# The first value product taken row tile by row tile of x, beside the norm of the next tile

## The chip, the cores and the metric

The kernel runs on one core of a Trainium2 chip. The metric is the device time of one execution in microseconds (us). Its engines are named as the profile names them: PE (TensorE, matmuls and transposes; PEld loads its weights), DVE (VectorE), ACT (ScalarE), POOL (GpSimd) and SP (SyncE, which here only issues transfers). Each engine runs its own queue in order, and waits at an instruction until the semaphores it needs have been raised.

## The reference

One decoder layer on x of 1024 tokens by 1024 features, in fp32. h = rms_norm(x) * pre_g; z = h @ w_in, whose columns are queries, keys, values and gates of 8 heads of differential attention (QA, KA, VA, GA) and of 4 heads of gated linear attention (QB, KB, VB, GB, and a narrow gate input); the two attentions; then out = x + rms_norm(mix @ w_out) * post_g. The change touches only the head of this: the norm of x, its transposition, and the first products of h with w_in.

```python
def hybrid_layer(x, layer_idx, pre_g, post_g, w_in, ...):
    h = rms_norm(x, pre_g)
    z = jnp.einsum('bsd,de->bse', h, w_in)
    qa, ka, va, ga, qb, kb, vb, gb, gk_low = split_columns(z)
    ...
```

## The kernel before

**Precision.** A matmul of two fp32 operands is done as three: each operand is split into a high part (rounded to the fast format, `hi`, by an ACT copy) and a rest (`lo`, by a DVE subtraction), and hi x hi, hi x lo and lo x hi are added in PSUM. So every weight block and every block of h passes ACT once and DVE once before PE may use it.

**Seven products for eight.** The product h @ w_in is done by a Strassen-like scheme on halves: seven products (numbers 1, 2, 6, 7, 5, 3, 4) of sums of blocks of h with sums of blocks of the weights. The blocks of h, all transposed so that features lie on partitions, are h11 (rows 0 to 511 of x, features 0 to 511), h12 (the same rows, features 512 to 1023), h22 (rows 512 to 1023, features 512 to 1023), and the sums s1 to s4. Product 1 needs h11, product 2 needs h12, product 6 needs s2, product 7 needs s3, product 5 s1, product 4 h22, product 3 s4.

**The order of work.** `order` lists the products by weight matrix: first the value matrix VB (512 columns at a time, called wide) in products 1 and 2, each in two steps kk over 256 features; then products 1 and 2 of three 256-column pairs of KA, QA (`EARLY`, their weights loaded at the head as `w_early`); then VB's products 6, 7, 5, 3, 4; then VA; then all else. `go(n)` takes the next n entries: it prepares the weights of the entries ahead (`prepare`, `make_weights`, `block_weights`) and issues the matmuls (`step`, `step_wide`, `multiply_wide`). A wide step is 24 matmuls of 128x512 into four PSUM banks, one for each row tile t of 128 tokens: 2 features blocks q by 3 terms j by 4 tiles.

**The head.** x lies in eight row tiles of 128 tokens. `norm_x(st)` for st 0 to 3 takes ACT's square with a sum, the inverse root (`rstd`: Ln and Exp on ACT, three small DVE steps), and the scaling of the tile by DVE (first half of the features) and POOL (second half). The four tiles' norms are issued one behind the other. `first(0)` transposes the first half of all four tiles on PE (16 transposes into four banks `xT`), and `put` makes h11's hi (ACT, times pre_g) and lo (DVE) from PSUM, 128x512 at a time; product 1 follows with all four row tiles for each feature block. `first(1)` does the same for h12. Tiles 4 to 7 are normed in pairs, scaled by POOL, and transposed in `blocks(j)`, four times, which makes h22, s2 and s3 for feature block j. `blocks` stands between steps of product 2 and of the first early pairs. POOL makes f1 (h11 and h12 in full precision, `f1hi` and `f1lo` in the profile), s1 and s4.

**What sets the order.** PE's instructions stay in program order (`mm`, `tr`). The instructions of other engines are placed by the framework's scheduler, unless `tc.keep_in_program_order` pins them or `tc.issue_after` puts them behind another. PSUM has eight banks, handed out by `take_bank` from the list `free` and given back in the order of release.

## Time and profile before

| | |
|---|---|
| median of 3 runs | 977.59 us (977.15 to 982.69) |
| the profiled execution | 977.73 us, span 976.0 us |
| PE busy | 956.0 us, 98% |
| DVE / ACT / POOL busy | 738.7 / 590.9 / 211.5 us |
| granted clock | 0.998 |

The span is the time from the first to the last recorded instruction; the execution's own time lies 1.7 us above it. A busy share is an average; where time can be won or lost is read from the stages: PE does its first transposes at 7.46 us, its first matmul at 13.71 us, and is then busy until the last slice.

### The profile page before, as it was taken

The page shows a single profiled execution, that of the slowest core. Times are in us where ns is not written, and L with a number is a line of the kernel's source. Part 1 is how long each engine was busy: PE and PEld are TensorE (multiplying, and loading weights), DVE is VectorE, ACT ScalarE, POOL GpSimd, SP SyncE. Part 2 cuts the span into 40 slices and gives each one's busy share as a digit, 9 for nine tenths or more (in the row PEclk, how much of TensorE's full clock was granted, in tenths as well). Part 3 has the DMA queues.
Part 4 walks back from the last instruction along what each step waited for, and adds up shares of the span by engine and source line. Part 5 has one row for each costly group of instructions (what it writes and reads, how often), then busy time and mean ns, then how long its engine had stood idle before and what let it go on. Part 6 is the DMA issues. An engine that isn't in the chain of part 4 may idle for free.

```text
span 976.0 us, 14803 instructions
## 1 busy us (share of the span) xinstructions
PE 956.0 (98%) x4866; PEld 806.1 (83%) x4866; DVE 738.7 (76%) x1450; ACT 590.9 (61%) x1152; POOL 211.5 (22%) x289
## 2 busy tenths in 40 slices
PE   6999999999999999999999999999999999999997
PEld 4888888878888888888888888788888888888875
DVE  6996476889889776778787766577787778887655
ACT  8641232347467467766677774357667667787764
POOL 5420100011211221112110000023232233443232
PEclk9999999999999999999999999999999999999999
DMA  8354643768865875899986569997575678995657
GB/s 306 99 152 153 212 134 98 217 174 270 265 240 194 268 250 192 265 280 304 315 278 183 180 204 346 376 337 233 164 252 185 189 267 246 331 262 104 194 157 156
DMA packets 144556, 220.37 MB, mean 226 GB/s; under 512 B 14704, under 2 KB 78704, under 8 KB 144384
## 3 DMA queue, kind: packets, MB, share of 16 engines
q1 hardware_dynamic: 130144, 175.38, 56.6%
q0 software_dynamic: 14336, 44.05, 15.1%
q8 instruction: 38, 0.62, 0.3%
q14 instruction: 38, 0.31, 0.1%
HBM read 133.93 MB, written 88.60 MB: 228 GB/s over the span
## 4 chain that ended last, share of the span: by engine, by line
PE 86%; DMA 6%; DVE 3%; ACT 3%; issue 1%; SPq 1%; DVEq 0%; POOL 0%; ACTq 0%
PE v L111 15%; PE x L111 15%; PE ypart L111 11%; PE y L111 10%; PE z L111 10%; PE sc L111 6%; PE po L111 5%; PE yps L111 4%; PE wtr L114 3%; PE gpo L111 2%; PE kv L111 1%; DMA m_raw<-mixd 1%; DMA m_lo<-mixe 1%; DMA mixd<-o 1%; DMA k_d<-qk_st 1%
## 5 line engine op out<-in xcount | busy, mean ns | idle before, releaser
L1177 ACT ACTIVATE p<-p,stt 128x896 f32<-128x896 f32 (+7 forms) x128 | 99.3, 777 | 46.7 <-DVE stt L1167 43.5
L335 DVE TENSOR_TENSOR w<-w_raw,w 128x512 fp32r<-128x512 f32 x134 | 91.9, 690 | 32.5 <-ACT w L333 32.1
L333 ACT CAST w<-w_raw 128x512 fp32r<-128x512 f32 x134 | 82.5, 620 | 42.9 <-PE y L111 19.9
L1203 POOL TENSOR_SCALAR p<-p,stt,lam 128x1024 f32<-128x1024 f32 (+3 forms) x64 | 55.7, 871 | 209.6 <-DVE stt L1202 203.9
L1167 DVE CUSTOM_DVE_ANT_0 p<-sc,maskt 128x512 f32<-128x512 f32 (+3 forms) x128 | 74.4, 585 | 33.2 <-PE sc L111 32.5
L111 PE MATMUL y<-h_hi,w 128*128 128x512 f32 x320 | 80.6, 394 | 0.0
L111 PE MATMUL x<-s_hi,w 128*128 128x512 f32 x320 | 80.5, 394 | 0.0
L111 PE MATMUL z<-s_hi,w 128*128 128x512 f32 x320 | 80.4, 393 | 0.0
L111 PE MATMUL ypart<-wo_hi,m_hi 128*128 128x512 f32 x192 | 79.5, 414 | 0.6 <-ACT yst L1384 0.5
L111 PE MATMUL v<-w,s_hi 128*128 128x512 f32 x256 | 79.0, 389 | 0.1
L111 PE MATMUL ypart<-wo_hi,m_lo 128*128 128x512 f32 x192 | 75.6, 394 | 0.7 <-DMA m_lo<-mixe 0.7
L111 PE MATMUL ypart<-wo_lo,m_hi 128*128 128x512 f32 x192 | 75.6, 394 | 0.5 <-DMA wo_lo<-wo_d 0.5
L488 ACT COPY s<-x 128x512 f32<-128x512 f32 x60 | 35.0, 584 | 65.2 <-PE x L111 65.0
L111 PE MATMUL sc<-k,q 128*128 128x512 f32 (+1 forms) x192 | 70.9, 372 | 0.4 <-DVE stt L1167 0.4
L111 PEld LDWEIGHTS z<-s_hi,w 128*128 128x128 f32 x320 | 59.1, 188 | 11.6
L111 PEld LDWEIGHTS x<-s_hi,w 128*128 128x128 f32 x320 | 59.1, 188 | 11.7
L111 PEld LDWEIGHTS y<-h_hi,w 128*128 128x128 f32 x320 | 59.0, 188 | 11.6
L111 PE MATMUL sc<-k,qs 128*128 128x512 f32 (+1 forms) x192 | 66.6, 349 | 0.0
L285 ACT CAST w<-w_block 128x1024 fp32r<-128x1024 f32 x24 | 25.0, 1051 | 65.3 <-PE v L111 42.3
L257 DVE TENSOR_TENSOR w_raw<-w_raw 128x512 f32<-128x512 f32 x80 | 55.3, 691 | 9.6 <-DMA w_raw<-in_w_in_dram 8.6
L111 PE MATMUL v<-w,h_hi 128*128 128x512 f32 x192 | 60.0, 400 | 0.4 <-ACT h_hi L582 0.4
L1207 DVE SCALAR_TENSOR_TENSOR p<-p,stt,p 128x1024 f32<-128x1024 f32 (+3 forms) x64 | 52.3, 819 | 6.7 <-POOL p L1203 6.5
(233 smaller groups left out, 2379.8 us busy)
## 6 DMA issues: line engine op xcount, KB each, us to landing
w_raw<-in_w_in_dram SPq DMA_DIRECT2D x40, 512.0 KB, 4.9
w_block<-in_w_in_dram SPq DMA_DIRECT2D x16, 512.0 KB, 4.4
wo_raw<-in_w_out_dram POOLq DMA_DIRECT2D x32, 256.0 KB, 4.2
wo_d<-wo_hi POOLq DMA_DIRECT2D x32, 256.0 KB, 4.5
wo_d<-wo_raw POOLq DMA_DIRECT2D x32, 256.0 KB, 5.0
qs<-q_d SPq DMA_DIRECT2D x32, 256.0 KB, 8.6
k<-k_d SPq DMA_DIRECT2D x16, 512.0 KB, 9.2
q<-q_d SPq DMA_DIRECT2D x16, 512.0 KB, 7.1
```

The costliest lines, as they stand in the source:

```text
L111: tc.keep_in_program_order(pe.matmul(*a, **k))
L114: tc.keep_in_program_order(pe.transpose(dst, src, ident))
L257: dve.tensor_tensor(dst, a, b, ALU.subtract)
L285: act.copy(w[0], src)
L333: act.copy(w[0], src)
L335: split_last[:] = [dve.tensor_tensor(w[1], src, fp(w[0]), ALU.subtract)]
L488: act.copy(b[k], ps)
L1167: ins = dve.tensor_tensor_reduce(p[:, a:e], sc[:, : e - a], maskt[:, NZ + P - (e - a) :] if last else maskt[:, : e - a], 1.0, 3e38 if i == ...
L1177: act.activation(p[:, :n], p[:, :n], AF.Exp, bias=st[:, m : m + 1], scale=-1.0, accum_out=st[:, 2 + m : 3 + m],)
L1203: pool.tensor_scalar(p1[:, :n], p1[:, :n], st[:, 5:6], lam, ALU.mult, ALU.mult)
L1207: dve.scalar_tensor_tensor(p0[:, :n], p0[:, :n], st[:, 4:5], p1[:, :n], ALU.mult, ALU.subtract)
```

## The change

It does five things.

1. Product 1 of VB is taken row tile by row tile (`first_product`): norm tile 0, transpose its first half, make 128 tokens of h11, multiply; then tile 1 and so on. The square of tile t+1 stands on ACT ahead of tile t's h_hi, and the norm of tile t+1 on DVE behind tile t's h_lo. The h11 pieces are 128x128 (16 on ACT, 16 on DVE) in the place of 128x512 (4 and 4). ACT's and DVE's instructions of this stretch are pinned. The weights' splits (`prepare(0)`, `prepare(1)`) stand between them.
2. The second half of the four tiles (`first`, h12) is transposed behind the matmuls of tile 2 and ahead of those of tile 3. f1lo, the full-precision h12, is made by POOL from hi and lo (`sum_parts`) and no longer by ACT from PSUM.
3. Row tiles 4 to 7 of x are loaded into the memory of the later block s1, so that the memory k0, k1, q0, q1 is free for the weights of product 6 at once; the loads of those (blocks 12 and 22 of VB) go to the head. The loads of x and of the first weights alternate.
4. Both steps of product 2 stand ahead of all four `blocks(j)`, which come between the steps of the early pairs; the norms of tiles 4 to 7 come behind h12.
5. The small loads (lambda vectors, sub_g, gla_g, bgk) are issued behind a late store of VB's values.

The core of the diff:

```diff
+    def squares(sts, ssq):
+        for i, st in enumerate(sts):
+            junk = hw.tile([P, D], F32, tag=("s2_hi0", "s2_lo0")[st % 2], name="junk")
+            yield act.activation(
+                junk, xs[st], AF.Square, scale=D**-0.5, accum_out=ssq[:, 0, i : i + 1]
+            )
...
+    def first_product(pss):
...
+        def square(st):
+            for ins in squares([st], ssq[st]):
+                kept(ins)
+
+        def scaled(st):
+            rstd(nc, ssq[st], ssq[st][:, 0], eps_t, kept)
+            norms[st] = ssq[st][:, 1]
+            kept(scale_x(st, cols(0), dve))
+
+        def turn(st):
+            ps, i = take_bank([P, HB, P], "xT")
+            for j in range(HB):
+                tr(ps[:, j], xs[st][:, j * P : j * P + P])
+            return ps, i
+
+        def out(st, ps, i):
+            cs = slice(st * P, st * P + P)
+            for j in range(HB):
+                g = pre_g[:, j : j + 1]
+                kept(act.activation(at(hi, j)[:, cs], ps[:, j], AF.Copy, scale=g))
+            for j in range(HB):
+                g = pre_g[:, j : j + 1]
+                kept(dve.scalar_tensor_tensor(
+                    at(lo, j)[:, cs], ps[:, j], g, fp(at(hi, j)[:, cs]), ALU.mult, ALU.subtract
+                ))
+            free.append(i)
+
+        def times(st, *ks):
+            for k in ks:
+                times_wide(pss[st], hi, lo, ws[k // 2], st, k, True)
+
+        square(0)
+        scaled(0)
+        prepare(0)
+        square(1)
+        t = turn(0)
+        out(0, *t)
+        times(0, 0, 1)
+        scaled(1)
+        prepare(1)
+        square(2)
+        t = turn(1)
+        out(1, *t)
+        times(0, 2, 3)
+        times(1, 0, 1, 2)
+        scaled(2)
+        square(3)
+        t = turn(2)
+        out(2, *t)
+        times(1, 3)
+        times(2, 0, 1, 2)
+        scaled(3)
+        t = turn(3)
+        out(3, *t)
+        times(2, 3)
+        for st in range(4):
+            scale_x(st, cols(1))
+        first()
+        norm_x(4, 5)
+        prepare(3)
+        norm_x(6, 7)
+        times(3, 0, 1, 2, 3)
...
-            xt = t_dec("xt")
+            tag = ("s1_hi0", "s1_hi1", "s1_lo0", "s1_lo1")[st - 4]
+            xt = hw.tile([P, D], F32, tag=tag, name="xt")
...
-            if h:
-                act.activation(f1[h][j], ps[j][0], AF.Copy, scale=pre_g[:, h * HB + j : h * HB + j + 1])
-            else:
-                pool.tensor_tensor(f1[h][j], fp(at(hi, j)), fp(at(lo, j)), ALU.add)
...
-    prepare(0)
-    first(0)
-    prepare(1)
     go(1)
-    first(1)
-    norm_x(4, 5)
-    norm_x(6, 7)
-    go(1)
+    with tc.issue_after(behind[1]):
+        sum_parts(1, "h12")
+    go(2)
     for j in range(HB):
         blocks(j)
         go(1)
```

**PE, the first rows.** x_189 holds row tiles 0 and 1, x_199 (x_192 before) tiles 2 and 3; xT is a PSUM bank of transposes, v the accumulators of product 1. Before:

```order
L114 MATMUL xT<-ident,x_189 128x128 x8
L114 MATMUL xT<-ident,x_192 128x128 x8
L111 MATMUL v<-w,h_hi 128x512 x8
L111 MATMUL v<-w,h_lo 128x512 x4
L111 MATMUL v<-w,h_hi 128x512 x8
L111 MATMUL v<-w,h_lo 128x512 x4
L114 MATMUL xT<-ident,x_189 128x128 x8
L114 MATMUL xT<-ident,x_192 128x128 x8
```

PE in the changed kernel, the first nine rows:

```order
L114 MATMUL xT<-ident,x_189 128x128 x4
L111 MATMUL v<-w,h_hi 128x512 x2
L111 MATMUL v<-w,h_lo 128x512
L111 MATMUL v<-w,h_hi 128x512 x2
L111 MATMUL v<-w,h_lo 128x512
L114 MATMUL xT<-ident,x_189 128x128 x4
L111 MATMUL v<-w,h_hi 128x512 x2
L111 MATMUL v<-w,h_lo 128x512
L111 MATMUL v<-w,h_hi 128x512 x2
```

Matmuls of tile 0 now stand ahead of tile 1's transposes; 15 (two blocks of tile 0, three of tile 1) stand between tile 1's and tile 2's.

**DVE, the first tiles.** ssq are the norm's small steps, x the scaling, h_lo the rest of h11, w<-w_block the rest of product 1's weights. Before, behind the first scaling:

```order
L1603 TENSOR_SCALAR ssq<-ssq,eps_t 128x1
L1605 SCALAR_TENSOR_TENSOR ssq<-ssq 128x1
L1611 SCALAR_TENSOR_TENSOR ssq<-ssq 128x1
L541 TENSOR_SCALAR x_189<-x_189,ssq 128x512
L1603 TENSOR_SCALAR ssq<-ssq,eps_t 128x1
L1605 SCALAR_TENSOR_TENSOR ssq<-ssq 128x1
```

DVE in the changed kernel, from the first weights on:

```order
L287 TENSOR_TENSOR w<-w_block,w 128x1024
L635 SCALAR_TENSOR_TENSOR h_lo<-xT,pre_g,h_hi 128x128 x4
L1684 TENSOR_SCALAR ssq<-ssq,eps_t 128x1
L1686 SCALAR_TENSOR_TENSOR ssq<-ssq 128x1
L1692 SCALAR_TENSOR_TENSOR ssq<-ssq 128x1
L550 TENSOR_SCALAR x_189<-x_189,ssq 128x512
L287 TENSOR_TENSOR w<-w_block,w 128x1024
L635 SCALAR_TENSOR_TENSOR h_lo<-xT,pre_g,h_hi 128x128 x4
```

Tile 1's norm and scaling now stand behind the weights of the first step and tile 0's four h_lo pieces.

**POOL, from f1hi to s1.** f1hi and f1lo are h11 and h12 in full precision, xt the row tiles 4 to 7, and the additions from s_446 (s_555) on make s1 and s4. Before:

```order
L606 TENSOR_TENSOR f1hi<-h_hi,h_lo 128x512 x4
L541 TENSOR_SCALAR xt<-xt,ssq 128x1024 x4
L640 TENSOR_TENSOR f1hi<-s_446,f1hi 128x512
L642 TENSOR_TENSOR s_446<-f1lo,s_446 128x512
L640 TENSOR_TENSOR f1hi<-s_504,f1hi 128x512
```

POOL in the changed kernel:

```order
L681 TENSOR_TENSOR f1hi<-h_hi,h_lo 128x512 x4
L550 TENSOR_SCALAR xt<-xt,ssq 128x1024 x4
L681 TENSOR_TENSOR f1lo<-h_hi,h_lo 128x512 x4
L728 TENSOR_TENSOR f1hi<-s_555,f1hi 128x512
L730 TENSOR_TENSOR s_555<-f1lo,s_555 128x512
```

Four additions f1lo are new on POOL, between the scaling of xt and the sums.

## The prediction

> **What bounds the kernel now.** First the page's shares and its slices:

> ```profile
> span 976.0 us, 14803 instructions
> ...
> PE 956.0 (98%) x4866; PEld 806.1 (83%) x4866; DVE 738.7 (76%) x1450; ACT 590.9 (61%) x1152; POOL 211.5 (22%) x289
> ...
> PE   6999999999999999999999999999999999999997
> ```

> TensorE (PE) works 956.0 of 976.0 us, and only its first and last slices have room. Time that PE loses anywhere is added to the end; time won at the head is taken off it. The waits of PE and the stages say how much room the head has:

> ```profile
> PE xT L114 <- DVE x L541: 8.9, 4, 7.5
> PE v L111 <- ACT h_hi L582: 0.4, 1, 0.4
> ```
> ```profile
> 7.40:13.70 6.30, 4.44 (x16) 2.87 (x16) 4.78 (x13) 6.11 (x15) 3.29 (x4) 1.00 1.02 362
> 28.00:40.00 12.00, 12.00 (x63) 10.17 (x62) 11.06 (x16) 7.04 (x13) 4.56 (x3) 1.00 0.16 46
> 40.00:60.00 20.00, 20.00 (x98) 16.75 (x97) 20.00 (x26) 10.71 (x18) 8.12 (x5) 1.00 0.59 196
> 60.00:100.00 40.00, 40.00 (x178) 33.11 (x178) 29.75 (x38) 12.03 (x14) 0.78 (x1) 1.00 0.48 136
> ```

> (Stage, length, then busy us of PE, PEld, DVE, ACT, POOL.) PE never waits from 13.71 to 100, so the most that can be won is part of the first 13.7 us. But in the stage 40 to 60 VectorE (DVE) is busy 20.00 of 20.00: it only just keeps ahead of PE. That is the second thing to watch.

> **The change, part by part.** The first tile runs thus before:

> ```profile
> 4.61 1.06 ACT L550 ACTIVATE junk<-x 128x1024 f32<-128x1024 f32 x1 [2.53 <-DMA x<-in_x_dram]
> ...
> 5.86 0.30 ACT L1601 ACTIVATE ssq<-ssq,eps_t 128x1 f32<-128x1 f32 x1
> ...
> 6.18 0.20 ACT L1602 ACTIVATE ssq<-ssq 128x1 f32<-128x1 f32 x1
> ...
> 6.42 0.22 DVE L1605 SCALAR_TENSOR_TENSOR ssq<-ssq 128x1 f32<-128x1 f32 x1 [0.33 <-ACT ssq L1602]
> ...
> 6.87 0.48 DVE L541 TENSOR_SCALAR x<-x,ssq 128x512 f32<-128x512 f32 x1
> ...
> 7.46 1.09 PE L114 MATMUL xT<-ident,x 128*128 128x128 f32 x4 [7.46 <-DVE x L541]
> ...
> 9.01 1.12 PE L114 MATMUL xT<-ident,x 128*128 128x128 f32 x4 [0.47 <-DVE x L541]
> ```

> Tile 0 of x was and is the first load; nothing stood before it, so I keep its transposes at 7.46. Tile 1 follows now in 1.55 us, because four norms run in a row. In the changed order a tile's DVE work is a chain kept in program order: four h_lo pieces of tile t, then the norm of t+1, its scaling, its transposes, its four h_hi pieces, its four h_lo pieces. The 128x128 pieces do not occur in the trace; these rows bound them:

> ```profile
> L1367 ACT CAST m_hi<-gate 128x128 fp32r<-128x128 f32 x8 | 2.3, 293 | 0.1
> ...
> L1368 DVE TENSOR_TENSOR m_lo<-gate,m_hi 128x128 fp32r<-128x128 f32 x8 | 2.3, 284 | 1.7 <-ACT m_hi L1367 1.7
> ```
> ```profile
> L583 DVE SCALAR_TENSOR_TENSOR h_lo<-xT,pre_g,h_hi 128x512 fp32r<-128x512 f32 x12 | 8.5, 739 | 0.0
> L582 ACT ACTIVATE h_hi<-xT,pre_g 128x512 fp32r<-128x512 f32 x12 | 7.6, 690 | 0.3 <-PE xT L114 0.3
> ```

> Below, 0.20 (the one-column L1602), above, 0.69 and 0.74; the nearest in shape are 0.29 and 0.28, which I take. One period is 4 x 0.29 (h_hi) + 4 x 0.28 (h_lo, which starts after the fourth h_hi) + 0.6 (three small norm steps of about 0.2) + 0.48 (scaling) + 0.7 (transposes, fast) + 0.25 (five handovers of 0.05) = 4.3 us; its bounds are 3.6 and 7.8. A tile's PE work is 12 matmuls and 4 transposes, 3.1 us at full rate, from these rows:

> ```profile
> 13.71 3.50 PE L111 MATMUL v<-w,h_hi 128*128 128x512 f32 x8 [0.38 <-ACT h_hi L582]
> ...
> 17.95 1.98 PE L111 MATMUL v<-w,h_hi 128*128 128x512 f32 x8
> ...
> 40.59 1.03 PE L114 MATMUL xT<-ident,xt 128*128 128x128 f32 x8
> 41.38 2.07 PE L111 MATMUL x<-h_hi,w 128*128 128x512 f32 x8
> 43.29 1.07 PE L111 MATMUL x<-h_lo,w 128*128 128x512 f32 x4
> ...
> 58.69 0.62 PE L111 MATMUL v<-w,s_hi 128*128 128x512 f32 x2
> ...
> 69.57 0.62 PE L111 MATMUL v<-w,s_hi 128*128 128x512 f32 x2
> ```

> From 58.69 to 69.57 stand 48 matmuls: 0.2267 each; eight transposes take 0.79 (40.59 to 41.38). The first eight matmuls took about 0.43 each: PE starts slow and is fast from some 17.1. In the window rows the granted clock is 1.00 all along, so it does not show this. [...]

> *Tiles.* Period one is longer: behind the Exp, ACT casts the first weights (1.05) and squares tile 1 (1.15) ahead of h_hi of tile 0, so h_hi ends at 9.8, h_lo at 11.0, and tile 1 is transposed at 12.2, not 9.01. DVE's second weight half ends at 13.3; from there PE has 15 matmuls ahead of tile 2's transposes. Taken slow for 3.4 us (8 of them) and then fast, they end at 18.3, while DVE's chain alone would allow 16.5. Tile 3 follows one period later, 22.6, and its h_lo ends at 25.7 (0.7 + 1.2 + 1.1 + handovers).

> *Behind the tiles.* The 16 transposes of h12 need the PSUM bank that tile 3's h_lo frees: 25.7 + 1.6 = 27.3. Then 12 matmuls of tile 3 (2.7) and the second value product, 48 (10.9): 41.0. Before, this point was 40.59 with 16 transposes of the last row tiles, 1.6, already done: PE is 2.0 late. Those transposes now wait for the norm of tiles 4 to 7, which before lay in ACT's idle room: behind h12's four h_hi (2.4, ending at 29.8) ACT has four squares, two norms, one cast and three early casts, 7.9, to 37.7; DVE's last norm steps are queued among the v_st additions, to 39.6; two scalings on POOL then end at 41.9.

> ```profile
> 24.64 2.24 POOL L541 TENSOR_SCALAR xt<-xt,ssq 128x1024 f32<-128x1024 f32 x2 [0.16 <-issue]
> ```

> So PE waits about 1 us and the blocks of h22, s2 and s3 begin 3 us late in PE's count; they also begin at 42, where they began at 27.9 before. Without further waits PE would reach the first matmul of product 6 at 42.1 + 3.2 (32 transposes) + 72 x 0.2267 = 61.6, against 58.69: **+2.9**.

> *DVE behind that.* Now its rate counts:

> ```profile
> 37.49 0.74 DVE L630 SCALAR_TENSOR_TENSOR s<-xT,pre_g,s 128x512 f32<-128x512 f32 x1
> 38.15 0.68 DVE L612 TENSOR_TENSOR s_lo<-s,s_hi 128x512 fp32r<-128x512 f32 x1
> 38.74 1.28 DVE L433 TENSOR_TENSOR v_st<-v,s 128x512 f32<-128x512 f32 x2
> ...
> 54.66 1.78 DVE L386 SCALAR_TENSOR_TENSOR qk_st<-s,qk_st 128x512 fp32r<-128x512 f32 x1
> ...
> 56.96 1.21 DVE L286 TENSOR_TENSOR w<-w_t,w 128x1024 fp32r<-128x1024 f32 x1
> 58.10 1.21 DVE L257 TENSOR_TENSOR w_block<-w_block 128x1024 f32<-128x1024 f32 x1
> 59.23 0.68 DVE L386 SCALAR_TENSOR_TENSOR qk_st<-s,qk_st 128x512 fp32r<-128x512 f32 x1
> ```
> ```profile
> L612 DVE TENSOR_TENSOR s_lo<-s,s_hi 128x512 fp32r<-128x512 f32 x8 | 7.1, 887 | 0.1
> ...
> L257 DVE TENSOR_TENSOR w_block<-w_block 128x1024 f32<-128x1024 f32 x4 | 5.4, 1342 | 0.0
> L335 DVE TENSOR_TENSOR w<-w_early,w 128x512 fp32r<-128x512 f32 x6 | 4.7, 791 | 0.1
> L386 DVE SCALAR_TENSOR_TENSOR qk_st<-s,qk_st 128x512 fp32r<-128x512 f32 x3 | 3.1, 1047 | 0.0
> ```
> ```profile
> 53.74 2.14 POOL L642 TENSOR_TENSOR s<-f1lo,s 128x512 f32<-128x512 f32 x1 [1.83 <-DVE s_lo L612]
> ```

> Start to start, DVE needs 0.66 for a multiply-subtract of 512, 0.60 for an addition, 1.13 for 1024 (37.49 to 38.15, 38.15 to 38.74, 58.10 to 59.23). Before, product 6's second weight half ended at 58.17 for a start at 58.69: half a microsecond of slack. In the changed order DVE has, from its first s3 at about 43.0 to the second weight half of product 6's second step, 14 of the first kind, 12 of the second, 6 of the third: 9.2 + 7.2 + 6.8 = 23.2. To that comes what POOL costs it. L386 took 1.78 beside a POOL addition that ended at 55.88, and 0.68 without one; over the four groups the excess on the undisturbed durations (0.68, 1.21, 0.68, 0.68) is 1.66 + 0.53 + 0.67 + 1.10 = 3.96 us for the eight POOL additions of L640 and L642, 0.5 each. The change adds four (f1lo, formerly four ACT passes) to this stretch: about 11 x 0.5 = 5.5. DVE is there at 71.7; PE wants it at 61.6 + 5.4 + 0.2 = 67.2: **+4.5**. With no such cost, +0 (66.2); with a whole POOL pass lost each time, some +10. Until product 7's first weights DVE has another 7.4 (four s1_lo, one 1024 subtraction, qk_st, three additions, one split) against 5.4 of PE: **+1.9**. From then DVE has room again (29.75 of 40).

> [...]

> *What costs nothing.* Loads: the four blocks for product 6 are asked for some 25 us earlier, in memory that the row tiles no longer hold; behind them on SP stands only the third early weight load, which waits for DVE in any case. The seven small loads (lambda, norms, bias) move behind a late value store of the first matrix, ahead of the next matrix's stores; their DVE steps, 1 us, then fall where DVE is busy 74%. Without that cover they would cost that 1 us.

> **Sum.** 2.9 + 4.5 + 1.9 = 9.3 us on the profiled execution, 977.73 (span 976.0 and 1.7 around it), which is 0.14 above the median of 977.59: **987.0 us**.

> **Rivals.** *The head is won* (the other side). If tiles overlap, period 3.1 as PE's work, PE has 48 matmuls and 32 transposes from about 9: 14.1 + 1.7 for the slow start, done at 24.8 instead of 27.9, so 974.6. It decides at a chain of 3.1 us per tile; the rows give 3.6 at the lowest. 7%. *DVE keeps up*: only the head is lost, 2.9 and at most 1.2 at product 7: 980.6 to 982. It needs the POOL cost near zero; 3.96 us in eight speaks against. 22%. *PE stays slow* until tile 3: 15 + 12 matmuls at 0.43 delay tile 3 by up to 3 us more, 990; some 5 us with hardly a gap from 13.3 speak against, as 3.4 were enough before. With a larger POOL cost, 17%. [...] *It does not do what it says*: if weights of tile 0 land late, PE starts later than 9; small, 2%.

> **How the numbers follow.** The forecast has 52%, for itself 983.5 to 990. The range 979.5 to 991 leaves out the head's win and the worst of the slow case, under 2 in 10. A measurement here can tell about 1%, 9.8 us, from no change: over 987.4 lie nearly half of the forecast and the slow rival, 40%; under 967.8 almost nothing, 2%; 58% within.

> **What would show it.** Transposes of tiles 1, 2, 3 at 12, 18, 22.6, against 9.01, 10.61, 12.21; 128x128 pieces of 0.28 us; PE waiting for the xt scaling near 41; DVE without gaps from 42 to 79; PE waits of 4 to 5 us in product 6's second step and 2 at product 7. Wrong would be: a tile period near 3, or DVE idle while PE runs products 6 and 7.

## The result, and the profile after

The changed kernel takes 991.27 us (median of 6 runs, 990.38 to 996.02) beside 979.54 us (6 runs) for the kernel before on the same chip: 1.0126 times as long, 95% interval 1.0097 to 1.0156. A second measurement of 5 rounds gave 1.0144 (1.0122 to 1.0166). The forecast was 987.0 with an upper end of 991.0: the direction and the places were right, the size was some 4 us too small, and the time lies just outside the range. The profiled execution took 990.65 us (977.73 before), and its 12.9 us more are what has to be found (between the medians it is 11.7).

The page of the changed kernel:

```profile
span 988.9 us, 14822 instructions
...
PE 960.6 (97%) x4866; PEld 806.3 (82%) x4866; DVE 742.6 (75%) x1462; ACT 589.6 (60%) x1160; POOL 217.8 (22%) x293
...
PE   5979999999999999999999999999999999999997
```

PE issues the same 4866 instructions and is busy 4.6 us longer, although nothing was added to its work; the other 8.3 us are idle time, 7.5 of them ahead of product 7 (the slices show 5, 9, 7, where before 6, 9, 9 stood). The waits of PE, with the total, the count and the longest:

```profile
PE xT L114 <- DVE x L550: 7.2, 1, 7.2
PE v L111 <- DVE w L287: 4.0, 3, 3.5
PE v L111 <- ACT h_hi L632: 1.6, 1, 1.6
PE gms L111 <- DVE gqd L1055: 1.6, 1, 1.6
PE xT L114 <- DVE h_lo L635: 1.4, 1, 1.4
PE y L111 <- DVE s L718: 1.0, 1, 1.0
...
PE v L111 <- DVE s L718: 0.5, 1, 0.5
...
PE xT L114 <- POOL xt L550: 0.4, 1, 0.4
```

Before, PE waited 8.9 us for the four scalings, now 7.2 for one. The 1.7 us won are given back in the head itself, with a wait of 1.58 for h_hi and one of 1.36 for the last h_lo, and 5.3 us of waits for DVE in the stage of the blocks (w twice, s twice) come on top. PE's rows (start, duration; in brackets the wait ahead and what ended it) show where:

```profile
7.17 1.09 PE L114 MATMUL xT<-ident,x 128*128 128x128 f32 x4 [7.17 <-DVE x L550]
9.83 1.22 PE L111 MATMUL v<-w,h_hi 128*128 128x512 f32 x2 [1.58 <-ACT h_hi L632]
...
12.92 0.72 PE L114 MATMUL xT<-ident,x 128*128 128x128 f32 x4
...
17.38 0.60 PE L114 MATMUL xT<-ident,x 128*128 128x128 f32 x4
...
24.59 1.64 PE L114 MATMUL xT<-ident,x 128*128 128x128 f32 x13 [1.36 <-DVE h_lo L635]
...
40.59 0.77 PE L114 MATMUL xT<-ident,xt 128*128 128x128 f32 x5 [0.38 <-POOL xt L550]
...
62.21 0.71 PE L111 MATMUL v<-w,s_hi 128*128 128x512 f32 x2 [0.50 <-DVE s L718]
...
72.19 0.80 PE L111 MATMUL v<-w,s_hi 128*128 128x512 f32 x1 [3.50 <-DVE w L287]
...
73.21 1.05 PE L111 MATMUL v<-w,s_hi 128*128 128x512 f32 x2
...
78.16 0.63 PE L111 MATMUL v<-w,s_hi 128*128 128x512 f32 x2
...
80.93 0.51 PE L111 MATMUL v<-w,s_hi 128*128 128x512 f32 x1 [0.30 <-DVE w L287]
```

The first matmul of a step needs only the high half of its weights (ACT's), the second is the first that needs the low half (DVE's). So the steps are compared by their second matmul; where a row holds two, it starts some 0.23 us behind the row's time. Product 6 starts at 62.21 (58.69 before), the second matmul of its second step stands at 72.19 (64.35 before), that of product 7 at 80.93 (69.79 before): 11.1 us later. Look at the durations behind the long wait: two matmuls take 1.05 us at 73.21 and 0.63 at 78.16. From 72.19 to 78.16 stand 14 matmuls, 0.426 us each, where 0.2267 was the rate before. PE ran at half rate, which makes 14 x 0.2 = 2.8 of the 4.6 us of added busy time. The windows (as before: length, busy PE, PEld, DVE, ACT, POOL, then the granted clock) say the same:

```profile
40.00:60.00 20.00, 18.61 (x97) 15.36 (x96) 19.98 (x22) 11.29 (x20) 12.72 (x9) 1.00 0.20 60
60.00:100.00 40.00, 35.42 (x141) 27.87 (x140) 31.77 (x40) 13.43 (x18) 6.63 (x5) 0.91 0.35 89
...
71.00:72.00 1.00, 0.00 (x0) 0.00 (x0) 1.00 (x1) 0.00 (x0) 0.05 (x1) 0.56 0.83 193
72.00:73.00 1.00, 0.81 (x2) 0.72 (x3) 1.00 (x3) 0.23 (x1) 0.00 (x0) 0.50 0.90 205
...
77.00:78.00 1.00, 1.00 (x4) 0.76 (x3) 0.71 (x2) 0.00 (x0) 0.39 (x1) 0.53 0.55 123
```

DVE is busy 19.98 of 20 us in the stage 40 to 60, as before, but PE is no longer covered by it. The granted clock is 0.50 in the one-us windows from 72 to 77; the shares 0.56 and 0.53 put its fall at 71.12 and its return at 77.94, 6.82 us later. The page's slices of 24 us are too coarse to show it.

DVE's rows on this path:

```profile
40.62 3.41 DVE L337 TENSOR_TENSOR w<-w_early,w 128x512 fp32r<-128x512 f32 x2
43.96 0.74 DVE L715 SCALAR_TENSOR_TENSOR s<-xT,pre_g,f1hi 128x512 f32<-128x512 f32 x1
...
45.94 2.74 DVE L700 TENSOR_TENSOR s_lo<-s,s_hi 128x512 fp32r<-128x512 f32 x2
...
69.86 2.28 DVE L287 TENSOR_TENSOR w<-w_t,w 128x1024 fp32r<-128x1024 f32 x1
```

The first s3 starts at 43.96 and the awaited weights end at 72.14: 28.2 us, where the sum had 28.7. The pairs at 40.62 and 45.94 took 3.41 and 2.74 us, for 1.28 undisturbed. Beside the first stand POOL's f1lo additions; beside the second stand the end of these and, from 46.39, the addition f1hi<-s, which was there before the change as well.

```profile
38.31 2.23 POOL L550 TENSOR_SCALAR xt<-xt,ssq 128x1024 f32<-128x1024 f32 x2 [3.37 <-ACT s L474]
40.49 5.94 POOL L681 TENSOR_TENSOR f1lo<-h_hi,h_lo 128x512 f32<-128x512 f32 x4
```

### The profile page after: what moved, and what is told of

Its sections match the earlier page's. It is cut to its first block, busy times and chain, and to the rows that moved or that the text cites. A ratio compares the mean times of both kernels' runs of the same rounds, so it can differ in the third digit from the quotient of the medians.

```text
span 988.9 us, 14822 instructions
## 1 busy us (share of the span) xinstructions
PE 960.6 (97%) x4866; PEld 806.3 (82%) x4866; DVE 742.6 (75%) x1462; ACT 589.6 (60%) x1160; POOL 217.8 (22%) x293
## 4 chain that ended last, share of the span: by engine, by line
PE 80%; DMA 10%; DVE 6%; ACT 2%; issue 2%; SPq 1%; DVEq 0%; POOL 0%; ACTq 0%
PE v L111 14%; PE x L111 13%; PE ypart L111 10%; PE y L111 9%; PE z L111 9%; PE sc L111 6%; PE po L111 5%; PE yps L111 4%; PE wtr L114 3%; PE gpo L111 2%; DMA mixe<-gg 1%; PE kv L111 1%; DMA q_d<-qk_st 1%; DMA q<-q_d 1%; DMA m_raw<-mixd 1%
## 5 line engine op out<-in xcount | busy, mean ns | idle before, releaser
L337 DVE TENSOR_TENSOR w<-w_raw,w 128x512 fp32r<-128x512 f32 x134 | 92.4, 692 | 33.1 <-ACT w L335 32.7
L335 ACT CAST w<-w_raw 128x512 fp32r<-128x512 f32 x134 | 82.4, 619 | 40.7 <-PE y L111 18.7
L111 PE MATMUL v<-w,s_hi 128*128 128x512 f32 x256 | 82.0, 401 | 4.9 <-DVE w L287 3.8
L111 PE MATMUL y<-h_hi,w 128*128 128x512 f32 x320 | 80.8, 395 | 1.0 <-DVE s L718 1.0
L111 PE MATMUL x<-s_hi,w 128*128 128x512 f32 x320 | 80.5, 394 | 0.0
L111 PE MATMUL z<-s_hi,w 128*128 128x512 f32 x320 | 80.4, 394 | 0.0
L111 PE MATMUL ypart<-wo_hi,m_hi 128*128 128x512 f32 x192 | 79.5, 414 | 0.6 <-ACT yst L1465 0.5
L111 PE MATMUL ypart<-wo_hi,m_lo 128*128 128x512 f32 x192 | 75.6, 394 | 0.7 <-DMA m_lo<-mixe 0.7
L111 PE MATMUL ypart<-wo_lo,m_hi 128*128 128x512 f32 x192 | 75.7, 394 | 0.0
L111 PE MATMUL sc<-k,q 128*128 128x512 f32 (+1 forms) x192 | 71.0, 372 | 0.4 <-DVE stt L1248 0.4
L111 PEld LDWEIGHTS y<-h_hi,w 128*128 128x128 f32 x320 | 58.9, 188 | 12.8 <-issue 1.2
L111 PEld LDWEIGHTS z<-s_hi,w 128*128 128x128 f32 x320 | 59.2, 188 | 11.7
L111 PEld LDWEIGHTS x<-s_hi,w 128*128 128x128 f32 x320 | 59.1, 188 | 11.7
L111 PE MATMUL sc<-k,qs 128*128 128x512 f32 (+1 forms) x192 | 66.6, 349 | 0.0
L286 ACT CAST w<-w_block 128x1024 fp32r<-128x1024 f32 x24 | 25.1, 1052 | 68.1 <-PE v L111 44.4
L111 PEld LDWEIGHTS v<-w,s_hi 128*128 128x128 f32 x256 | 49.1, 193 | 17.6 <-DVE w L287 4.5
L111 PE MATMUL v<-w,h_hi 128*128 128x512 f32 x192 | 61.1, 399 | 1.8 <-ACT h_hi L632 1.6
```

The costliest lines, as they stand in the source:

```text
L111: tc.keep_in_program_order(pe.matmul(*a, **k))
L286: in_order(act.copy(w[0], src))
L335: act.copy(w[0], src)
L337: split_last[:] = [dve.tensor_tensor(w[1], src, fp(w[0]), ALU.subtract)]
```

## The experiments

The theory after the first comparison: the three terms of the sum are there, and what they lack is PE's half rate behind the 3.50 us wait. Its rivals: POOL's f1lo costs DVE more than 0.5 us each; the blocks moved behind product 2 (part 4) cost more than the sum says; the tile chain or the norms of tiles 4 to 7 are late. The time of an execution scatters by some 2 us for a reason behind the change (below), so the start of product 7 in the profile (its second matmul) is the finer reading. It scatters too: product 6 starts at 62.21, 63.21 and 62.65 in three profiles of the same changed kernel, where the clock first rises to full rate at 13.10, 15.77 and 13.43 (the last section says how this is placed). So differences under some 1 us are not told apart. All times in us; "gms" is PE's wait for `gms` near 500 us, which is not part of the change.

| run | median | ratio to before (95%) | product 7, second matmul | gms |
|---|---|---|---|---|
| before | 977.59 | | 69.79 | 0.5 |
| after | 991.27 | 1.0126 (1.0097 to 1.0156) | 80.93 | 1.6 |
| r1_after_again | 991.26, one run | | 80.86 | 1.8 |
| r2_after | 989.99 | 1.0144 (1.0122 to 1.0166) | 81.31 | 1.1 |
| e1_no_f1lo | 988.24 | 1.0116 (1.0085 to 1.0147) | 77.64 | 2.6 |
| e2_filled | 986.69 | 1.0098 (1.0061 to 1.0134) | 78.79 | 0.5 |
| e2b_filled | 989.96 | 1.0130 (1.0114 to 1.0146) | 78.89 | 1.4 |
| e3_blocks_back | 994.79 | 1.0170 (1.0130 to 1.0210) | 80.06 | 4.0 |
| e4_before_p2_first | 984.99 | 1.0075 (1.0050 to 1.0100) | 72.92 | 1.8 |
| e5_short_chain | 990.43 | 1.0125 (1.0110 to 1.0140) | 82.06 | none |
| e6_f1lo_early | 990.29 | 1.0122 (1.0106 to 1.0138) | 80.73 | 1.7 |
| e7_chain_xt | 990.58 | 1.0136 (1.0117 to 1.0155) | 81.67 | 0.2 |
| e8_norm_early | 991.23 | 1.0134 (1.0103 to 1.0165) | 82.57 | 0.6 |
| e9_as_before_behind | 986.06 | 1.0092 (1.0067 to 1.0116) | 78.76 | 0.8 |
| e11_f1lo_act | 986.31 | 1.0082 (1.0063 to 1.0102) | 78.99 | 2.4 |
| e12_f1hi_behind | 985.42 | 1.0086 (1.0064 to 1.0108) | 75.33 | 3.8 |
| e10_loads_alone | 981.93 | 1.0044 (1.0025 to 1.0063) | 74.40 | 1.8 |
| e13_x_first | 977.62 | 1.0008 (0.9993 to 1.0023) | 70.45 | 2.8 |

### Is it the half rate? e1, e2, and the repeats

**e1_no_f1lo**, from the changed kernel:

```diff
-    with tc.issue_after(behind[1]):
-        sum_parts(1, "h12")
...
-            pool.tensor_tensor(s2[j], f1[1][j], s2[j], ALU.subtract)
+            pool.tensor_tensor(s2[j], f1[0][j], s2[j], ALU.subtract)
```

> The changed kernel without POOL's four f1lo additions (40.49 to 46.43 us in its trace); the s4 subtractions read f1hi in place of f1lo, so the output is not the reference's. Nothing else in the order of the head moves. Theory (POOL's additions stretch DVE's work beside them, and all of DVE's delay reaches PE): the two early splits (3.41 us for the pair) and the two s_lo splits (2.74) fall back towards their undisturbed 1.28 a pair, 3 us in all; PE's wait of 3.50 us at product 6's second step falls to 0.5 or less, the granted clock of 60 to 80 us returns to 1.00, product 7 starts at about 75 instead of 80.93, and the time is 985 to 986 us against 991.3. Rival (DVE is late only because its blocks start later; POOL costs it nothing): the wait stays at 3 us or more and the time at 990 to 991.5. Rival (DVE loses a whole pass for each addition): 5 us of DVE, no wait left, 984 or less.

From the start of the early weights' split (L337) to the end of product 6's second weights DVE needed 29.0 us instead of 31.5: the four additions cost 2.5 us, 0.63 each, near the 0.5 of the sum. Nearly all of it is the early pair, back at 1.28; the s_lo pair still took 2.38. The theory expected a shorter wait of PE. It did not get shorter, since PE too came 1.75 us earlier to that place: the time, 988.24, lies between the theory and its rival, and product 7 is 3.3 us earlier. Behind the same wait PE was fast:

```profile
70.43 0.50 PE L111 MATMUL v<-w,s_hi 128*128 128x512 f32 x1 [3.50 <-DVE w L287]
70.76 0.40 PE L111 MATMUL v<-w,s_lo 128*128 128x512 f32 x1
71.00 0.62 PE L111 MATMUL v<-w,s_hi 128*128 128x512 f32 x2
...
77.64 0.50 PE L111 MATMUL v<-w,s_hi 128*128 128x512 f32 x1 [1.48 <-DVE w L287]
```

Here the third term of the sum is seen by itself: from 70.43 to 77.64 are 7.21 us, 1.8 more than before the change (5.44), forecast 1.9; 1.48 of it is one wait. So a wait of 3.50 us does not always bring the half rate, which e1 was not made to show; the last section compares where the two waits lay.

**e2_filled** puts 15 matmuls of no use into the wait:

```diff
+        if (kind, n, kk) == ("VB", 6, 1):
+            ps, b_free = take_bank([P, 512], "fill")
+            for _ in range(FILL):
+                mm(ps, ones, at(H["h11"][0], 0), start=True, stop=True)
+            free.append(b_free)
```

> The changed kernel with 15 extra matmuls of 128x512 into an unused PSUM bank ahead of product 6's second step, 3.4 us of work in place of most of the 3.5 us wait; their result is not used. Theory (PE falls to half rate because it stood idle for 3.5 us): the 24 matmuls behind the wait run at 0.227 us instead of the 0.43 of the first fourteen, the granted clock of 60 to 80 us is 1.00, and product 7 starts at 78 instead of 80.93: 988 to 989 us against 991.3. Rival (the slow stretch is hidden, as DVE sets the start of product 7 in any case): granted clock 1.00, but product 7 still at 80.5 to 81 and 991. Rival (the slow stretch has another cause than idleness): the granted clock stays near 0.83 and the time is 991 or more.

```profile
69.46 3.73 PE L111 MATMUL fill<-h_hi,ones 128*128 128x512 f32 x15 [0.99 <-DVE s L513]
73.03 0.62 PE L111 MATMUL v<-w,s_hi 128*128 128x512 f32 x2
...
78.49 0.80 PE L111 MATMUL v<-w,s_hi 128*128 128x512 f32 x2
```

The second matmul of the step starts 1.1 us later than in the changed kernel (73.26 against 72.19), and that of product 7 2.1 us earlier. +9.0 us against before remain there. That is near the sum's +9.3, but not by its terms: +8.9 at the step, and no wait at product 7. And the half rate is not all that the filler took away. On DVE the framework placed one of the additions s<-v ahead of product 7's weights,

```profile
76.93 0.68 DVE L482 TENSOR_TENSOR s<-v,s 128x512 f32<-128x512 f32 x1
77.53 1.21 DVE L287 TENSOR_TENSOR w<-w_block,w 128x1024 fp32r<-128x1024 f32 x1
```

where e1 and the changed kernel have three: two additions less, 1.2 us. So e2 shows that behind the filled wait the full rate was kept (granted clock 1.00 from 60 to 80, 0.83 in r2), but not what the half rate costs. **r1_after_again** is the changed kernel once more:

> The changed kernel unchanged, a second look. Theory (PE's fall to half rate behind the 3.5 us wait depends on where the wait lies in the clock's own windows, since an equally long wait in the run without f1lo left the rate at 0.227 us a matmul): the wait is 3.4 to 3.6 us again, the rate behind it may be 0.43 or 0.227 us, and product 7's start moves with it between 79 and 81 us. Rival (the fall belongs to the program): 14 matmuls at 0.43 again.

The same wait of 3.50, but only some 8 slow matmuls, from 73.8 to 77.2, half as long as before. **r2_after** and **e2b_filled** are both kernels again, side by side in 5 rounds:

> The changed kernel again, as the other side of the filled run below: 990 to 992 us; mean granted clock 0.993 to 0.997 in most executions, where PE falls to half rate behind the wait.

> The changed kernel with 15 extra matmuls in the wait, again. Theory (the fall to half rate costs 2 to 3 us at product 7's start): 2 to 4 us less than the changed kernel beside it, granted clock 0.998 or more in every execution. Rival (the first gain was the scatter of executions): within 1 us of it.

Product 7 is at 81.31 and 78.89: 2.4 us earlier with the filler, 1.2 of it again two additions less on DVE. End to end the two are not told apart (989.99 and 989.96), and the granted clock was 0.996 to 0.998, not 0.998 or more: e2b's profile has a half-rate spell at another place, from 643.16 to 646.56. A gain at product 7 is shown twice, a gain in the time is not.

What the half rate costs there can be read from the changed kernel's own three profiles and e1, which has the same order on DVE. From the second step's second matmul to that of product 7 PE took 8.74 (after) and 8.69 us (r2) with a slow spell of 6.82 us, 7.67 (r1) with one of 3.42, and 7.21 (e1) with none. So the long spell costs 1.5 us at product 7 and the short one 0.5. Its 14 slow matmuls lose 2.8, but DVE would have kept PE waiting for part of that in any case.

### Where DVE's lateness comes from: e3, e4, e6

**e3_blocks_back** undoes one half of part 4's move: of product 2's two steps, one stands ahead of the blocks (two in the changed kernel, none before it):

```diff
-    go(2)
+    go(1)
     for j in range(HB):
         blocks(j)
         go(1)
+    go(1)
     sums_of("s1")
```

> The changed kernel with part 4 undone: the four blocks calls start again behind the first step of product 2, as before the change. Theory (what is late is xt, the scaled tiles 4 to 7, at about 40.5 us, and with it DVE's block work; where the blocks stand on PE does not matter): PE waits some 4 to 5 us for xt near 36 us, DVE's work from the first s3 to product 6's second weights is the same 26 us and some 5 of POOL's cost, so it ends near 72 to 73 as now: 990 to 993 us. Rival (the place of the blocks is the cause): 984 to 987 us, with little or no PE wait at product 6.

Product 7 is at 80.06, 0.9 us earlier, which is within the scatter. With the blocks between product 2's steps PE meets them before tiles 4 to 7 are normed. Waits of PE in this run:

```profile
PE xT L114 <- ACT s L474: 2.2, 1, 2.2
PE xT L114 <- POOL xt L550: 2.1, 2, 1.5
```

and the clock falls to 0.50 from 37.3 to 44.1. The time is longer (994.79), but the intervals overlap, and the profile is 5.7 us longer behind product 7, with a wait of 4.0 at gms and a second half-rate spell behind it. So taking the blocks back alone wins next to nothing: PE waits for the late norms instead of for DVE's weights.

**e4_before_p2_first** makes half of that move alone, in the kernel before: the edit puts one step of product 2 ahead of the blocks, while its expectation speaks of both:

```diff
-    go(1)
+    go(2)
     for j in range(HB):
         blocks(j)
         go(1)
...
     load_blocks("VB", "12", "22")
-    go(1)
```

> The kernel before with one thing of part 4 alone: both steps of product 2 ahead of the blocks; the head with its four norms, 512-wide h11 and xt done by 27 us stays. Theory (a late start of DVE's block work is the cost, whatever delays it): the blocks begin at about 41.5 us, DVE has 37 instructions, 28 us undisturbed and 4 beside POOL, to product 6's second weights, so these end at 70 to 74 against the 64.3 that PE wants; PE waits 5 to 9 us, falls to half rate behind the wait, and the time is 984 to 990 us. Rival (the tile chain of the head is the cost): 977 to 980 us.

```profile
33.14 1.03 PE L114 MATMUL xT<-ident,xt 128*128 128x128 f32 x8
```

The blocks begin at 33.14 (27.92 before), not at the 41.5 of the theory. Product 7 is 3.1 us later (72.92 against 69.79), with waits for DVE's weights of 1.83 in product 6's first step and 0.52 at product 7. So half of the move costs 3.1 us in the old head; the whole was not run. Since e3, which takes half of it back in the changed kernel, wins only 0.9, the parts do not add up, and the 11.1 us at product 7 cannot be shared out among the order, the head, the norms and f1lo.

**e6_f1lo_early** spreads f1lo: two additions ahead of the second pair of xt scalings:

```diff
         norm_x(4, 5)
+        with tc.issue_after(behind[1]):
+            sum_parts(1, "h12", 0, 1)
...
-        sum_parts(1, "h12")
+        sum_parts(1, "h12", 2, 3)
```

> The changed kernel with two of POOL's four f1lo additions moved ahead of the last scaling of xt, into a stretch in which POOL waits and DVE has room (28 to 42 us, DVE busy 10.8 of 14.0); the other two stay behind it. Theory (an addition on POOL costs DVE some 0.6 us where DVE has no room, nothing where it has): half of what the run without f1lo won, 1.2 us at product 7's start: 988.5 to 990.5 us. Rival (it is the pair of early splits beside the first two additions that suffers, 2.1 of the 2.5 us): the two additions that stay meet the same splits, and nothing is won, 991. Rival (xt's last scaling comes later by the two additions, 2.6 us, and with it the blocks): 993.

The wait for product 6's second weights fell from 3.50 to 2.09, but PE now waits 1.62 and 1.72 us for xt at 42 and 44: what DVE won, the scalings lost. Product 7 is 0.2 earlier, which is nothing.

### Can the chain be shortened? e5, e7

**e5_short_chain** puts the square and norm of tile t+1 between tile t's h_hi and its h_lo, and tile t+1's transposes ahead of more of the matmuls:

```diff
+        highs(0, t[0])
         square(1)
-        t = turn(0)
-        out(0, *t)
-        times(0, 0, 1)
         scaled(1)
+        lows(0, *t)
+        times(0, 0, 1)
         prepare(1)
```

> The changed kernel with the tile chain cut shorter and nothing else moved: on ACT a tile's h_hi pieces stand ahead of the next tile's square for tiles 0 and 1, on DVE the next tile's norm and scaling stand ahead of the tile's h_lo pieces, on PE the transposes of tiles 2 and 3 stand one to two matmul groups earlier. Theory (the head loses to the chain of a tile's pieces and the next tile's norm, and all that is behind it, DVE's block work too, is late by as much): transposes of tiles 1, 2, 3 at about 12, 16 and 18 us against 12.92, 17.38 and 21.54, the second product of the values ends at about 36.5 instead of 41.1, the blocks start 4 to 5 us earlier, DVE's lag behind PE at product 6 stays 3 to 4 us, product 7 starts at 75 to 77 instead of 80.93: 984 to 987 us. Rival (DVE's lag alone sets product 7, so an earlier head only makes PE wait longer there): the wait at product 6 grows to 7 us or more and the time stays above 989.

The tiles' transposes came at 7.11, 14.54, 20.69 and 22.53, h12's at 25.73 (24.59 in the changed kernel). PE waited 1.82 us for h_lo at 12.67 and 1.38 at 19.66: tile 0's h_hi was done at 9.8, but DVE came to its h_lo at 12.27, behind the norm of tile 1, which waits for ACT's square. The clock, too, rose only at 17.30 (13.10 to 15.77 in the changed kernel), so PE's first matmuls were slow for longer; how much of the delay is that was not separated. A miss. **e7_chain_xt** is e5 with the casts of the early weights behind the last norm of tiles 4 to 7, and with e3's order of the blocks:

```diff
-        act.copy(w[0], src)
+        with tc.issue_after(behind[0]) if p < EARLY and n < 3 else nullcontext():
+            act.copy(w[0], src)
```

> The changed kernel with the short tile chain, the casts of the early weights put behind the norm of tiles 6 and 7 on ACT (so that DVE's last norm step no longer stands behind the v_st additions), and the blocks again behind the first step of product 2. Theory (the time is set by when DVE can start its block work, here at about 32 us instead of 43, and 28 at the earliest in the kernel before): PE waits up to 2 us for xt near 31 us, DVE reaches product 6's second weights at 63 to 65, product 7 starts at 69 to 72 against 80.93 now and 69.57 before: 977 to 981 us. Rival (f1lo on POOL and the 128x128 pieces cost DVE too much in any order): 984 us or more.

Also a miss: PE waits 1.57 and 1.81 us for xt and 0.77 for ACT from 37 to 41, and the clock first rose at 18.94. Three things were changed at once here, so nothing is shown of any one of them.

### The norms of tiles 4 to 7: e8, e9, e11, e12

**e8_norm_early** moves them into ACT's idle time between the first tiles (the copies s<-v of product 1 then stand behind h12's first h_hi, no longer behind the last norm):

```diff
         scaled(3)
+        norm_x(4, 5)
         t = turn(3)
...
             scale_x(st, cols(1))
+        norm_x(6, 7)
         first()
-        norm_x(4, 5)
         prepare(3)
-        norm_x(6, 7)
```

> The changed kernel with the norms of tiles 4 to 7 moved on ACT into the gaps of the tile chain (ahead of the last tile's h_hi, and ahead of the second half's h_hi), where ACT stood idle for 1.7, 2.7 and 1.6 us, and nothing moved on PE. Theory (two things together make DVE late: xt comes late, and the blocks stand behind both steps of product 2; taking away one of them alone wins nothing): xt is scaled by about 33 us instead of 40.5, but PE reaches the blocks at 41 us as before, DVE's block work starts within 1 us of the present 43.96, product 7 starts at 80 to 82: 989 to 992 us. Rival (xt's lateness alone was the cause): product 7 at 76 or earlier, 986 or less.

The time is the theory's (991.23), product 7 a little later than it said (82.57), and for another reason: xt is ready, but h12's h_lo is late, and PE waits 3.02 us for it at 33.73. **e9_as_before_behind** is e8 with blocks, products and s1 in the order of before:

```diff
-    go(2)
     for j in range(HB):
         blocks(j)
         go(1)
-    sums_of("s1")
     go(1)
+    sums_of("s1")
+    go(2)
```

> The same early norms, and the blocks in their old places too: one ahead of each step of product 2 and of the first two early products. Product 1 stays by row tiles, f1lo stays on POOL. Theory (the time follows the start of DVE's block work): first s3 at 30 to 32 us against 29.05 in the kernel before and 43.96 in the changed one; PE waits 1 to 2 us for h_hi near 28 us; product 7 starts at 72 to 75 us: 980 to 984 us. Rival (the tile chain and f1lo on POOL are the cost wherever the blocks stand): 987 us or more.

A miss: product 7 is at 78.76 and not at 72 to 75, the first s3 at 36.68 and not at 30 to 32, and the time, 986.06, lies between theory and rival. The rows of DVE in e9 show why h_lo is late:

```profile
23.31 0.16 DVE L1692 TENSOR_TENSOR ssq<-ssq 128x2 f32<-128x2 f32 x1 [0.19 <-ACT ssq L1685]
...
27.61 1.14 DVE L1692 TENSOR_TENSOR ssq<-ssq 128x2 f32<-128x2 f32 x1
28.79 1.22 DVE L1693 TENSOR_TENSOR ssq<-ssq 128x2 f32<-128x2 f32 x1
30.04 1.19 DVE L1694 SCALAR_TENSOR_TENSOR ssq<-ssq 128x2 f32<-128x2 f32 x1
...
32.28 2.71 DVE L594 SCALAR_TENSOR_TENSOR h_lo<-xT,pre_g,h_hi 128x512 fp32r<-128x512 f32 x4
```

and POOL's:

```profile
26.20 5.01 POOL L681 TENSOR_TENSOR f1hi<-h_hi,h_lo 128x512 f32<-128x512 f32 x4
...
34.41 6.88 POOL L681 TENSOR_TENSOR f1lo<-h_hi,h_lo 128x512 f32<-128x512 f32 x4
```

Three norm steps of two columns take 0.16 us alone and 1.14 to 1.22 beside f1hi, the length of one POOL addition (5.01 for four). The h_lo at 32.28, which read one operand from PSUM, take 0.66 each start to start, as before, beside POOL's scaling of xt; in the changed kernel the same four, from 26.66, take 2.73 us together beside f1hi. **e11_f1lo_act** makes f1lo by ACT again, in e9:

```diff
+        with tc.issue_after(behind[0]):
+            for j in range(HB):
+                act.activation(f1[1][j], ps[j][0], AF.Copy, scale=pre_g[:, HB + j : HB + j + 1])
...
-    with tc.issue_after(behind[1]):
-        sum_parts(1, "h12")
```

> As the run with early norms and the blocks in their old places, and with f1lo made by ACT from PSUM as before the change. Theory: four POOL additions less, 2.5 us of DVE less, but four ACT passes of 0.6 us more ahead of the second step's weights; product 7 starts at 70 to 73 us, up to 2 us earlier than with f1lo on POOL: 978 to 982 us. If it comes under 976, product 1 by row tiles is won by itself and only what stands behind it was lost. Rival (ACT becomes the bound near 30 us): the same as, or above, the run with f1lo on POOL.

No gain (product 7 at 78.99): the wait is f1hi's, not f1lo's, and PE waits 3.79 us for xt, which stands behind f1hi on POOL. **e12_f1hi_behind** is e11 with f1hi behind the xt scalings:

```diff
-        sum_parts(0, "h11")
+        with tc.issue_after(behind[1]):
+            sum_parts(0, "h11")
```

> The run with early norms, the blocks in their old places and f1lo on ACT, with one thing more: POOL's four f1hi additions stand behind the scaling of xt, no longer beside the norm steps of tiles 6 and 7. Theory (a DVE instruction with two inputs in SBUF, however small, waits for a whole POOL addition): these four steps fall from 0.97, 1.14, 1.21 and 1.19 us to about 0.2 each, 3.5 us together; h12's h_lo pieces start at 28.5 to 29.5 instead of 32.85, PE's wait of 3.79 us ahead of the blocks falls to 1 or less, product 7 starts 3 us earlier: 982 to 984 us against 986.3. Rival (POOL's cost is half a microsecond an addition wherever it stands): f1hi costs the instructions that it now meets as much, 985 to 987 us.

```profile
27.05 0.16 DVE L1694 TENSOR_TENSOR ssq<-ssq 128x2 f32<-128x2 f32 x1 [0.33 <-ACT ssq L1687]
27.24 0.16 DVE L1695 TENSOR_TENSOR ssq<-ssq 128x2 f32<-128x2 f32 x1
...
29.88 2.71 DVE L594 SCALAR_TENSOR_TENSOR h_lo<-xT,pre_g,h_hi 128x512 fp32r<-128x512 f32 x4
```

The steps are at 0.16 again, h_lo starts 2.4 us earlier than in e9, and product 7 is 3.7 earlier than in e11. PE's wait ahead of the blocks is still 2.94, now for f1hi itself. In the time the gain is not seen (985.42 and 986.31, the rival's range): behind product 7 e12's profile is 4.0 us longer than e11's, with a wait of 3.8 at gms and half rate from 502.64 to 509.48 behind it. It is the best of the changed versions at product 7, still 5.5 us behind the kernel before, and no version beats that kernel.

### The loads: e10, e13

**e10_loads_alone** is the kernel before with parts 3 and 5. The head of its loads:

```diff
-    for st in range(4):
-        load_x(st)
+    load_x(0)
     sp.dma_start(pre_g, pre_norm_g[0].rearrange("(k p) -> p k", p=P))
...
-    load_blocks("VB", "11")
+    for st in range(1, 3):
+        load_block("VB", "11", st - 1)
+        load_x(st)
+    load_x(3)
```

> The kernel before with parts 3 and 5 alone: tiles 4 to 7 in the memory of s1, the blocks 12 and 22 loaded at the head, x and the first weights loaded in turn, the small loads behind a value store. Theory (these cost nothing of their own, since all four norms of the head still wait for the fourth tile): x of tiles 1 to 3 lands up to 2.5 us later behind the first weights, so the first matmul may come 1 us later than 13.71: 977 to 980 us. Rival (the alternation delays the third and fourth tile enough to move everything): 981 or more. Rival (early weights help DVE ahead of product 6): 976 or less.

ACT's square of tile 1, and PE's first matmul, which before started at 13.71:

```profile
9.21 1.06 ACT L556 ACTIVATE junk<-x 128x1024 f32<-128x1024 f32 x1 [3.29 <-DMA x<-in_x_dram]
...
17.57 3.78 PE L111 MATMUL v<-w,h_hi 128*128 128x512 f32 x8 [0.38 <-ACT h_hi L593]
```

The loads are not free in the old order of work: 1.0044 times the time of before, the first matmul 3.9 us later. **e13_x_first** is e10 with the four row tiles ahead of all weights, as before (the early blocks 12 and 22, the memory of s1 and the late small loads stay); against e10:

```diff
-    load_x(0)
+    for st in range(4):
+        load_x(st)
...
-    for st in range(1, 3):
-        load_block("VB", "11", st - 1)
-        load_x(st)
-    load_x(3)
+    load_blocks("VB", "11")
```

> The kernel before with tiles 4 to 7 in the memory of s1, the blocks 12 and 22 loaded early and the small loads late, but with the loads ahead of these in their old order: x of tiles 0 to 3 first. Theory (the 4 us of the run with the loads alone are the order alone, which brought x of tile 1 at 9.2 us instead of 6.3): first matmul at 13.7 us again, 977 to 979 us. Rival (the early blocks crowd out later loads): 980 or more. Rival (the early weights and the absent small steps give DVE room): 975 to 976.

First matmul at 13.74, time as before within 0.2%. So e10's loss is the alternation of x and weights; the rest of parts 3 and 5 costs nothing that the time shows. (Product 7 is 0.7 later in this profile, as product 6 is; the clock rose at 18.18 here and at 16.75 in the kernel before.) The changed kernel with x loaded first was not run.

## Why the prediction was right and wrong

| point | predicted | measured |
|---|---|---|
| transposes of tiles 1, 2, 3 | 12.2, 18.3, 22.6 | 12.92, 17.38, 21.54 |
| 128x128 pieces of h_hi, h_lo | 0.29, 0.28 | 0.28, 0.28 (four in 1.12 and 1.13) |
| product 6 starts, against before | +2.9 | +3.5 |
| its second step (second matmul), against before | +7.4 | +7.8 |
| product 7 (second matmul) | +9.3 | +11.1 |
| end of the span | +9.3 | +12.9 |

**Right.** The chain per tile (4.2 to 4.5 us a tile, 4.3 forecast) and with it that the head wins nothing that lasts; that DVE, not PE, sets product 6's second step, at 72.14 (71.7 forecast); that f1lo on POOL costs DVE about half a microsecond each (e1: 0.63); a short wait for xt (0.38, 1 forecast); that the small late loads, the s1 memory and the early blocks cost nothing that the time shows (e13). The +0.6 at product 6 is partly a wait of 1.00 and one of 0.50 for DVE's s, against a product 2 that ended at 39.72 and not 41.0.

The 3.6 us that the sum lacks in the profile are 0.6 at product 6, -0.2 at its second step, 1.4 in the third term and 1.8 behind product 7.

**Wrong: the third term.** The sum let PE wait 1.9 us for DVE at product 7 and run at full rate until there. Measured are 3.3 (from 72.19 and 64.35 to 80.93 and 69.79), with only 0.30 of it a wait: PE spent 72.19 to 77.94 at half rate. 1.8 of the 3.3 are DVE's, as e1 shows at full rate, and 1.5 the half rate. (At the prediction's own rates DVE's items there add up to 7.1 and not 7.4, which would be +1.6.) The prediction counted slow matmuls (0.43 each) only at the start; at this place it forecast a wait of 4 to 5 us, with full rate behind it. Where the wait itself comes from is read from DVE's order and not tested: the weights' split (L287 at 69.86) stands behind s_lo, s and qk_st. An earlier place for it was not tried.

**Wrong: nothing behind product 7.** The sum took the rest as unchanged. It is 1.8 us longer in the profiled execution (908.0 and 906.2), 1.1 of it the wait at gms, which differs from execution to execution of any of these kernels: from none to 4.0 in the table, and 0.5 to 2.8 among the versions of the kernel before. What sets it stays open, beyond that ACT's first step of a gate waits there for the q_d stores to land (1.11 us before, 1.89 after, 3.34 in e12). Where it is longest (e3, e12, e13), a half-rate spell follows it. That it has nothing to do with the change fits the table but is not shown; it hides 2 us won or lost at product 7 from the time.

**Wrong: "Loads".** The part on what costs nothing priced only the early blocks. The alternation of x and weights costs 3.9 us in the old head (e10). In the changed kernel tile 1 was forecast 0.7 us too early, and its x is squared at 8.37 (6.29 before); whether any of that reaches product 6 was not tested.

Of the rivals, "PE stays slow until tile 3" did not come (the matmuls from 14.4 are fast: an h_lo matmul takes 0.39 at 14.39, and 0.63 at 12.43); the half rate came behind the wait at product 6 instead. "DVE keeps up" and "the head is won" are refuted by the 3.50 us wait. A longer slow start does occur: in e5 and e7 PE stayed slow until 17.30 and 18.94.

## What to carry to other kernels

When a sum says that PE will wait some 2 us or more (in these profiles PE was idle for 1.93 to 3.04 us in the 3.41 ahead of each fall), price the half rate behind the wait as well: here 2.8 us of PE time, of which 1.5 reached product 7. It came in all three profiles of the changed kernel and not in e1's; the granted clock by the microsecond shows it (0.50 from 72 to 77), the page's slices of 24 us do not. A head made finer only pays if the engine that is full behind it (here DVE, 20 of 20 us) gets its work no later. Before judging by the time of the whole, find a start in the trace (here product 7) that lies behind the change and ahead of most of the scatter, and compare the same matmul in both.

## What the runs showed of the hardware

**The clock fell on a grid.** Each fall and return, read as at 71.12 and 77.94 from one-us windows of the granted clock, with PE's idle time in the 3.41 us ahead of the fall:

| run | slow from, to | length | idle in the 3.41 us ahead |
|---|---|---|---|
| after | 71.12, 77.94 | 6.82 | 2.70 |
| r1_after_again | 73.80, 77.22 | 3.42 | 2.80 |
| r2_after | 71.46, 78.28 | 6.82 | 2.59 |
| e2b_filled | 643.16, 646.56 | 3.40 | 1.93 |
| e3_blocks_back | 37.30, 44.12; 511.74, 515.16 | 6.82; 3.42 | 2.20; 1.93 |
| e5_short_chain | 71.92, 78.74 | 6.82 | 2.10 |
| e6_f1lo_early | 44.44, 47.84 | 3.40 | 2.91 |
| e7_chain_xt | 39.42, 46.24 | 6.82 | 2.49 |
| e8_norm_early | 33.96, 37.38; 74.92, 78.34 | 3.42; 3.42 | 3.02; 1.97 |
| e9_as_before_behind | 33.10, 39.94 | 6.84 | 3.04 |
| e11_f1lo_act | 33.14, 39.96 | 6.82 | 2.51 |
| e12_f1hi_behind | 502.64, 509.48 | 6.84 | 2.11 |
| e13_x_first | 499.46, 502.88 | 3.42 | 2.01 |

Every slow spell in the table lasted one or two times 3.41 us: one (r1, e2b, e6, e8, e13, the second of e3) where PE was busy all through it, two where 0.5 to 2.1 us of its first half were idle. The spells followed stretches with 1.93 to 3.04 us idle; waits of 3.50 (e1), 2.94 (e12) and 2.09 (e6, at 73.52) brought none.

The traces show where the difference lies. Within an execution the falls and returns lay whole multiples of one length apart: in e8 the falls at 33.96 and 74.92 are 40.96 us apart, 12 x 3.413; in the changed kernel the fall at 71.12 and the last one, where the program ends, at 985.90, are 914.78 apart, 268 x 3.4134. The spells of the table, 23 such lengths in 78.50 us, give 3.413 as well. So a fall is taken to place the borders of its whole execution. e1 has only the one at its end, which this window puts at 983.38 (before the granted clock: length, busy PE, PEld, DVE, ACT, POOL):

```profile
983.00:984.00 1.00, 0.00 (x0) 0.00 (x0) 0.36 (x1) 0.00 (x0) 0.00 (x0) 0.69 0.45 176
```

**Small DVE steps took about as long as the POOL additions beside them.** The 128x2 steps of e9 (0.16 alone, 1.14 to 1.22 beside POOL's f1hi, whose four additions took 5.01) are the clearest case; in e12, with f1hi behind them, the same steps took 0.16 each. In the sum's stretch the cost came to 0.63 us per addition (e1) and not to the whole 1.29 that POOL's s<-f1lo took at 48.82: the two early splits, with both inputs in SBUF, lost 2.1 us together (3.41 for 1.28), and the three operations behind them, which read PSUM, kept their 0.66 beside f1lo.
